# Latent attention's query projection without duplicated rotary columns, in a two-layer transformer trunk on one Trainium2 core

## The chip, the core and the metric

The kernel runs on one core of a Trainium2 chip. The core's engines run instruction streams of their own: PE (TensorE) multiplies matrices and transposes, DVE (VectorE), ACT (ScalarE) and POOL (GpSimd) work on tiles element by element, SP (SyncE) issues the DMAs. They wait for one another by semaphores. The metric is the device time of one execution in microseconds (us).

## The reference

Two layers over 256 tokens of 1024 numbers, all in fp32. Each layer mixes tokens in two groups of eight heads (latent attention and a sparse attention), then does a cross attention and a gated feed-forward. What matters here is the latent attention:

```python
q = (rms_norm(cq, cq_g) @ w_uq).reshape(B, S, 8, 64 + 32)
q_nope = q[..., :64]
q_rope = apply_rope(q[..., 64:], cos, sin)
s = (einsum('bqhd,bkhd->bhqk', q_nope, k_nope)
     + einsum('bqhd,bkd->bhqk', q_rope, k_rope)) * 96 ** -0.5

def apply_rope(x, cos, sin):
    x1, x2 = split(x, 2, axis=-1)          # 16 and 16
    return concatenate([x1 * c - x2 * s, x1 * s + x2 * c], axis=-1)
```

The query projection `w_uq` has 384 rows and 8 x 96 columns; the rotated part of the key is one for all heads.

## The kernel before

Every fp32 product is made of three matmuls: each operand is split into a high part (`hi`, by ACT, L130) and the rest (`lo`, by DVE, L131, which reads the raw tile and the high part), and hi x hi, lo x hi and hi x lo are added in PSUM (L177 to L179 where the weights stand still and the tokens move, L169 to L171 the other way). Weights come in by DMA, a piece at a time, into four raw buffers; the split pieces turn in six `hi` and six `lo` buffers.

A layer's attention is a list of named steps, written out by hand for each layer; the instructions of each step go to the engines in the order in which a list scheduler puts them, fixed before the run. In the two layers the end of the list reads

```
layer 0: ch qk3 kr mq2 mq0 fill mkv par2 mq1 mq3 av3 mqk2 mqk3 mqk0 mqk1 mav0 mav1 fill mav3 mav2
layer 1: ch av2 qk3 kr mq0 mkv mq3 mq1 av3 mqk0 mq2 mqk1 mqk3 mav0 mav3 mqk2 mav1 mav2
```

`mq0` to `mq3` (`mla_q`) project the queries of two heads each into `qT[g]`, where g is the group of four heads: pairs 0 and 1 make group 0, pairs 2 and 3 group 1. `mkv` makes keys (`kT`) and values, `kr` the rotary part of the keys. `mqk0` to `mqk3` (`mla_qk`, L721 and L722) are the scores and softmax of two heads each, `mav` their product with the values. `av3` is the last step of the sparse attention: transpositions of its probabilities (`pt`, L561), copies of them to SBUF (tag `pT`, four buffers, L564 on ACT and L566 on DVE), and products with the values (`pv`, L570 and L571, with `vsl` and then `vwn`). `fill` is work of the cross attention (keys and values of the memory), placed among the rest.

In `mla_q` a head takes 128 columns: 64 without rotation, the 32 rotary ones, and the two rotary halves of 16 once more, swapped. Each pair of heads has one raw piece of 3 x 192 columns, three splits on ACT and three on DVE into 3 x 256 columns, two chains of nine matmuls of 128x256, and one multiplication on DVE (L713) by the table `c_cs`, which holds ones, cosines and sines. The scores then contract over all 128 rows: the keys carry their rotated 32 rows twice (L404), so the product adds the two halves of the rotation.

## Time and profile before

| what | value |
|---|---|
| time of three runs, median (lowest to highest) | 888.48 us (885.98 to 889.66) |
| profiled execution, span | 887.0 us |
| mean granted clock of PE | 0.995 |
| matmuls of a query projection (L177 to L179, tile `mla`) | 18 per pair of heads, 72 per layer |
| multiplications by `c_cs` (L713) | 8 |
| POOL's instructions | 60 |

The profiled execution is one run of its own; the profile gives its span from the first to the last instruction and no other time for it. Busy times in a profile are sums over instructions, and matmuls overlap in the records, so that what a matmul takes in a sequence is read from the chain or from the starts. An engine's row in a window says how much of that stretch it worked.

### The profile page before, as it was taken

The page shows a single profiled execution, that of the slowest core. Times are in us where ns is not written, and L with a number is a line of the kernel's source. Part 1 is how long each engine was busy: PE and PEld are TensorE (multiplying, and loading weights), DVE is VectorE, ACT ScalarE, POOL GpSimd, SP SyncE. Part 2 cuts the span into 40 slices and gives each one's busy share as a digit, 9 for nine tenths or more (in the row PEclk, how much of TensorE's full clock was granted, in tenths as well). Part 3 has the DMA queues.
Part 4 walks back from the last instruction along what each step waited for, and adds up shares of the span by engine and source line. Part 5 has one row for each costly group of instructions (what it writes and reads, how often), then busy time and mean ns, then how long its engine had stood idle before and what let it go on. Part 6 is the DMA issues. An engine that isn't in the chain of part 4 may idle for free.

```text
span 887.0 us, 15857 instructions
## 1 busy us (share of the span) xinstructions
PE 857.6 (97%) x6088; PEld 794.2 (90%) x6088; DVE 659.9 (74%) x1293; ACT 511.7 (58%) x938; POOL 44.8 (5%) x60
## 2 busy tenths in 40 slices
PE   3999999999999999999999999999999999999996
PEld 3989798899989999999989998879998899999995
DVE  6788887766587777677687788868566877767767
ACT  4669764545545565465555678636573476555551
POOL 1053100000000000000000020000000000000000
PEclk9999999999999999999999999999999999999998
DMA  8954463485247656556537734546633746656631
GB/s 243 301 154 122 130 188 99 144 260 166 95 143 238 190 178 208 184 167 206 176 119 199 216 90 109 143 131 212 192 116 110 236 149 205 200 161 188 214 122 48
DMA packets 128523, 149.76 MB, mean 169 GB/s; under 512 B 6289, under 2 KB 111039, under 8 KB 128447
## 3 DMA queue, kind: packets, MB, share of 16 engines
q1 hardware_dynamic: 128447, 148.75, 54.6%
q8 instruction: 48, 0.79, 0.4%
q14 instruction: 28, 0.23, 0.1%
HBM read 147.68 MB, written 1.05 MB: 168 GB/s over the span
## 4 chain that ended last, share of the span: by engine, by line
PE 88%; DVE 5%; DMA 3%; ACT 2%; issue 1%; SPq 0%; POOL 0%; DVEq 0%; ACTq 0%; POOLq 0%
PE up L179 9%; PE up L178 9%; PE up L177 9%; PE acc L947 4%; PE acc L948 4%; PE acc L949 4%; PE acc L170 3%; PE acc L169 3%; PE acc L171 3%; PE fill L171 2%; PE xq L179 2%; PE xq L178 2%; PE xq L177 2%; PE fill L169 2%; PE fill L170 2%; PE pt L561 2%
## 5 line engine op out<-in xcount | busy, mean ns | idle before, releaser
L131 DVE TENSOR_TENSOR lo<-raw,hi 128x1024 fp32r<-128x1024 f32 (+5 forms) x296 | 320.6, 1096 | 82.9 <-ACT hi L130 78.3
L130 ACT ACTIVATE hi<-raw 128x1024 fp32r<-128x1024 f32 (+5 forms) x296 | 279.7, 957 | 152.7 <-PE acc L171 34.6
L179 PE MATMUL up<-xTh,lo 128*128 128x256 f32 x672 | 190.2, 283 | 0.0
L178 PE MATMUL up<-xTl,hi 128*128 128x256 f32 x672 | 190.2, 283 | 0.0
L177 PE MATMUL up<-xTh,hi 128*128 128x256 f32 x672 | 190.2, 283 | 0.0
L178 PEld LDWEIGHTS up<-xTl,hi 128*128 128x128 f32 x672 | 128.9, 192 | 0.7
L177 PEld LDWEIGHTS up<-xTh,hi 128*128 128x128 f32 x672 | 128.9, 192 | 0.7
L179 PEld LDWEIGHTS up<-xTh,lo 128*128 128x128 f32 x672 | 128.9, 192 | 0.0
L931 DVE SCALAR_TENSOR_TENSOR cv<-up,par,cv 128x255 f32<-128x255 f32 x88 | 42.1, 479 | 51.6 <-ACT cv L930 51.5
L930 ACT ACTIVATE cv<-up,par 128x256 f32<-128x256 f32 x88 | 49.0, 559 | 52.6 <-PE up L179 48.0
L948 PE MATMUL acc<-lo,frh 128*128 128x512 f32 x176 | 68.8, 391 | 0.0
L947 PE MATMUL acc<-hi,frh 128*128 128x512 f32 x176 | 68.7, 392 | 0.0
L949 PE MATMUL acc<-hi,frl 128*128 128x512 f32 x176 | 68.2, 389 | 0.0
L548 ACT ACTIVATE p<-p,nm 128x128 f32<-128x128 f32 (+1 forms) x96 | 42.8, 450 | 9.5 <-DVE nm L545 9.3
L199 POOL TENSOR_TENSOR mv<-mv,mhalf 128x1 f32<-128x1 f32 x16 | 14.7, 920 | 650.5 <-DVE mv L223 497.6
L932 DVE SCALAR_TENSOR_TENSOR cv<-up,par,cv 128x254 f32<-128x254 f32 x88 | 42.0, 479 | 1.4
L937 ACT ACTIVATE frh<-cv 128x256 fp32r<-128x256 f32 x44 | 18.3, 419 | 37.8 <-DVE cv L935 37.6
L949 PEld LDWEIGHTS acc<-hi,frl 128*128 128x128 f32 x176 | 33.0, 188 | 7.5 <-DVE frl L938 0.6
L947 PEld LDWEIGHTS acc<-hi,frh 128*128 128x128 f32 x176 | 33.1, 188 | 6.9 <-ACT frh L937 0.8
L177 PE MATMUL projt<-xTh,hi 128*128 128x256 f32 x128 | 37.2, 292 | 1.9 <-DVE c2l L462 1.6
L948 PEld LDWEIGHTS acc<-lo,frh 128*128 128x128 f32 x176 | 33.1, 188 | 6.0
L178 PE MATMUL projt<-xTl,hi 128*128 128x256 f32 x128 | 37.0, 289 | 0.5 <-DVE xTl L240 0.5
(257 smaller groups left out, 2027.6 us busy)
## 6 DMA issues: line engine op xcount, KB each, us to landing
raw<-in_ffn_w_up SPq DMA_DIRECT2D x88, 512.0 KB, 4.9
raw<-in_ffn_w_down SPq DMA_DIRECT2D x44, 512.0 KB, 4.3
raw<-in_xa_wkv SPq DMA_DIRECT2D x32, 512.0 KB, 4.3
raw<-in_xa_wq SPq DMA_DIRECT2D x16, 512.0 KB, 4.6
raw<-in_xa_wo SPq DMA_DIRECT2D x16, 512.0 KB, 4.1
raw<-in_w_in SPq DMA_DIRECT2D x24, 256.0 KB, 4.8
raw<-in_w_out SPq DMA_DIRECT2D x16, 256.0 KB, 5.4
raw<-in_w_out SPq DMA_DIRECT2D x8, 512.0 KB, 5.1
```

Source lines behind the costliest of these rows:

```text
L130: A.activation(h_, x_, AF.Copy)
L131: V.tensor_tensor(l_, x_, h_.bitcast(F32), op=ALU.subtract)
L169: T.matmul(o, xh_[:, t, k], h, start=k == 0, stop=False)
L170: T.matmul(o, xh_[:, t, k], lo, start=False, stop=False)
L171: T.matmul(o, xl_[:, t, k], h, start=False, stop=k == len(ws) - 1)
L177: T.matmul(o, h[:, ms], xh_[:, :, k], start=k == 0, stop=False)
L178: T.matmul(o, h[:, ms], xl_[:, :, k], start=False, stop=False)
L179: T.matmul(o, lo[:, ms], xh_[:, :, k], start=False, stop=k == len(ws) - 1)
L930: A.activation(c, u, AF.Identity, bias=pcol("cb", l, ft), scale=w_[2])
L947: T.matmul(o, fh[:, ts_], h[:, cs_], start=f == 0, stop=False)
L948: T.matmul(o, fh[:, ts_], lo[:, cs_], start=False, stop=False)
L949: T.matmul(o, fl[:, ts_], h[:, cs_], start=False, stop=f == NF - 1)
```

## The change

The duplicated columns go. A pair of heads projects its 2 x 64 columns without rotation in nine matmuls, and the 4 x 32 rotary columns of a group of four heads form one tile of 128 columns of their own, projected in nine matmuls by the second pair of the group. Their split weights (`rhi`, `rlo`) are filled in two halves, one by each pair, and hold a `hi` and a `lo` buffer from the first pair to the second. The 64 rows of each head go from PSUM to `qT` by a copy (ACT for one head of the pair; for the other DVE in a group's first pair and ACT in its second). The rotary tile is rotated by a shuffle of the partitions by 16 within each block of 32 (DVE), a multiplication by the cosines (`rc`, DVE), one of the shuffled tile by the signed sines (`rs`, POOL), and four additions of 32x256, in turn on POOL and DVE. `rc` and `rs` are buffers of the tag `pT`. The scores contract over 96 rows, the keys carry the rotated rows once, and `c_cs` has two tables of 256 columns.

```diff
-    cs = np.ones((P, S), f)
-    cs[64:80], cs[80:96] = cos.T, cos.T
-    cs[96:112], cs[112:128] = -sin.T, sin.T
+    cs = np.stack([np.tile(np.concatenate([cos.T, cos.T]), (4, 1)), np.tile(np.concatenate([-sin.T, sin.T]), (4, 1))], 1)
...
-                G.tensor_copy(kr[:, t, 96:128], kr[:, t, 64:96])
...
-                    V.tensor_copy(kT[g][64:128], pb[64:128, None, 0:S].to_broadcast([64, 4, S]))
+                    V.tensor_copy(kT[g][64:96], pb[64:96, None, 0:S].to_broadcast([32, 4, S]))
...
         def mla_q(ch, hp):
-            r2 = lambda v: v.rearrange("p k (h c) -> p (k h) c", h=2)
-            cols = [(lambda v: r2(v), lambda v: r2(v)[:, :, 0:96]),
-                    (lambda v: r2(v)[:, :, 80:96], lambda v: r2(v)[:, :, 96:112]),
-                    (lambda v: r2(v)[:, :, 64:80], lambda v: r2(v)[:, :, 112:128])]
-            ws = wmat(a["mla_w_uq"][l], [(hp * 192, (hp + 1) * 192)], ks=3, cols=cols, wn=256)
+            g, i = divmod(hp, 2)
+            last = g in rw
+            if not last:
+                rw[g] = [wp.tile([P, 3, P], F32R, name="r" + s, tag=s, bufs=HL) for s in ("hi", "lo")]
+            rh, rl = rw[g]
+            r = wp.tile([P, 1024], F32, name="raw", tag="raw", bufs=RAW)
+            rv = r[:, :576].rearrange("p (k n) -> p k n", k=3)
+            nc.sync.dma_start(rv, a["mla_w_uq"][l][:, hp * 192:(hp + 1) * 192].rearrange("(k p) n -> p k n", p=P))
+            h, lo = [wp.tile([P, 3, P], F32R, name=s, tag=s, bufs=HL) for s in ("hi", "lo")]
+            heads = lambda v: v.rearrange("p k (h c) -> p k h c", h=2)
+            ms = slice(64 * i, 64 * i + 64)
+            for cut, dh, dl in ((slice(0, 64), h, lo), (slice(64, 96), rh[:, :, ms], rl[:, :, ms])):
+                src, dh, dl = heads(rv)[:, :, :, cut], heads(dh), heads(dl)
+                A.activation(dh, src, AF.Copy)
+                V.tensor_tensor(dl, src, dh.bitcast(F32), op=ALU.subtract)
             pb = bank("mla")
-            for i in range(2):
-                mm_tr(pb[:, i * S:(i + 1) * S], ch[0], ch[1], ws, i * P)
-            j = 2 * (hp % 2)
-            V.tensor_tensor(qT[hp // 2][:, j:j + 2, :], pb.rearrange("p (i n) -> p i n", i=2),
-                            cs[:, None, :].to_broadcast([P, 2, S]), op=ALU.mult)
+            mm_tr(pb[:, 0:S], ch[0], ch[1], [(h[:, k], lo[:, k]) for k in range(3)], 0)
+            if last:
+                mm_tr(pb[:, S:2 * S], ch[0], ch[1], [(rh[:, k], rl[:, k]) for k in range(3)], 0)
+            A.activation(qT[g][0:64, 2 * i, :], pb[0:64, 0:S], AF.Copy)
+            copy_(qT[g][0:64, 2 * i + 1, :], pb[64:128, 0:S], i)
+            if last:
+                del rw[g]
+                rc, rs = [tmp.tile([P, S], F32, name=n, tag="pT", bufs=4) for n in ("rc", "rs")]
+                V.stream_shuffle(rs, pb[:, S:2 * S], [(c + 16) % 32 for c in range(32)])
+                V.tensor_tensor(rc, pb[:, S:2 * S], cs[:, 0], op=ALU.mult)
+                G.tensor_tensor(rs, rs, cs[:, 1], op=ALU.mult)
+                for j in range(4):
+                    js = slice(32 * j, 32 * j + 32)
+                    (G, V)[j % 2].tensor_tensor(qT[g][64:96, j, :], rc[js], rs[js], op=ALU.add)
...
-                T.matmul(b0[:, 0:P], qT[g][:, j, 0:P], kT[g][:, j, 0:P], start=True, stop=True)
-                T.matmul(b0[:, P:P + S], qT[g][:, j, P:S], kT[g][:, j, :], start=True, stop=True)
+                T.matmul(b0[:, 0:P], qT[g][0:96, j, 0:P], kT[g][0:96, j, 0:P], start=True, stop=True)
+                T.matmul(b0[:, P:P + S], qT[g][0:96, j, P:S], kT[g][0:96, j, :], start=True, stop=True)
```

The order moves with it at three places. First DVE in layer 0, between the projections `mq1` and `mq3` and the first softmax step (L545, in the changed kernel L542). Before; the splits `lo` of 128x1024 belong to the output weights:

```order
L131 TENSOR_TENSOR lo<-raw,hi 128x1024
L713 TENSOR_TENSOR qT_1340<-mla,c_cs 128x512
L131 TENSOR_TENSOR lo<-raw,hi 128x1024
L713 TENSOR_TENSOR qT_1341<-mla,c_cs 128x512
L131 TENSOR_TENSOR lo<-raw,hi 128x1024
L566 COPY pT<-pt 128x384
L131 TENSOR_TENSOR lo<-raw,hi 128x1024
```

After:

```order
L129 TENSOR_TENSOR lo<-raw,hi 128x1024 x2
L728 STREAM_SHUFFLE rs<-mla 128x256
L729 TENSOR_TENSOR rc<-mla,c_cs 128x256
L733 TENSOR_TENSOR qT_1338<-rc,rs 32x256 x2
L129 TENSOR_TENSOR lo<-raw,hi 128x1024
L728 STREAM_SHUFFLE rs<-mla 128x256
L729 TENSOR_TENSOR rc<-mla,c_cs 128x256
L733 TENSOR_TENSOR qT_1339<-rc,rs 32x256 x2
L563 COPY pT<-pt 128x384
L129 TENSOR_TENSOR lo<-raw,hi 128x1024
```

Two splits now stand together ahead of the rotation of group 0, a third between the two rotations, and one behind the copy `pT`; each rotation ends in two additions that read what POOL has multiplied.

Second POOL in layer 0, from the key's rotary part to the statistics of the next layer norm (L199, after L197). Before:

```order
L631 MEMSET pc 128x512
L402 MEMSET kr 128x64 x2
L199 ISA
L199 TENSOR_TENSOR mv<-mv,mhalf 128x1 x2
L447 MEMSET kk_160 64x512
```

After:

```order
L400 MEMSET kr 128x64 x2
L730 TENSOR_TENSOR rs<-rs,c_cs 128x256
L733 TENSOR_TENSOR qT_1338<-rc,rs 32x256 x2
L730 TENSOR_TENSOR rs<-rs,c_cs 128x256
L733 TENSOR_TENSOR qT_1339<-rc,rs 32x256 x2
L197 TENSOR_TENSOR mv<-mv,mhalf 128x1 x2
```

POOL had nothing to do between the two; now a multiplication and two additions for each group of heads stand there.

Third PE in layer 1, from the last projection `mq2` to the scores of heads 6 and 7 (`mqk3`). Before, `qT_6439` and `qT_6440` being the two groups' queries:

```order
L178 MATMUL mla<-xTl,hi 128x256
L179 MATMUL mla<-xTh,lo 128x256
L721 MATMUL mqk<-kT_6441,qT_6439 128x128
L722 MATMUL mqk<-kT_6441,qT_6439 128x256
L721 MATMUL mqk<-kT_6441,qT_6439 128x128
L722 MATMUL mqk<-kT_6441,qT_6439 128x256
L721 MATMUL mqk<-kT_6442,qT_6440 128x128
L722 MATMUL mqk<-kT_6442,qT_6440 128x256
L721 MATMUL mqk<-kT_6442,qT_6440 128x128
L722 MATMUL mqk<-kT_6442,qT_6440 128x256
```

After, where the groups are `qT_6435` and `qT_6436`:

```order
L175 MATMUL mla<-xTh,rhi 128x256
L176 MATMUL mla<-xTl,rhi 128x256
L177 MATMUL mla<-xTh,rlo 128x256
L740 MATMUL mqk<-kT_6437,qT_6435 128x128
L741 MATMUL mqk<-kT_6437,qT_6435 128x256
L740 MATMUL mqk<-kT_6437,qT_6435 128x128
L741 MATMUL mqk<-kT_6437,qT_6435 128x256
L558 MATMUL pt<-c_ident,p 128x128 x6
L740 MATMUL mqk<-kT_6438,qT_6436 128x128
L741 MATMUL mqk<-kT_6438,qT_6436 128x256
L740 MATMUL mqk<-kT_6438,qT_6436 128x128
```

The scores of group 1 came after two heads of group 0; now six transpositions stand there too, and these scores read the rotation of the tile that the nine `rhi` and `rlo` matmuls ahead have made.

## Rows read from the trace of the kernel before

**Rows 1.** Page, part 1: busy us of each engine, its share, instructions.

```profile
PE 857.6 (97%) x6088; PEld 794.2 (90%) x6088; DVE 659.9 (74%) x1293; ACT 511.7 (58%) x938; POOL 44.8 (5%) x60
```

**Rows 2.** Waits of PE, whole program: total us, times, longest.

```profile
PE pt L561 <- ACT pT L564: 1.7, 3, 0.8
```

**Rows 3.** Windows, layer 0: start:end us, busy by engine, granted clock, DMA share, GB/s.

```profile
110.00:117.00 7.00, 7.00 (x61) 7.00 (x60) 6.94 (x20) 3.71 (x9) 0.00 (x0) 1.00 0.08 11
117.00:128.00 11.00, 11.00 (x84) 10.23 (x84) 8.50 (x13) 7.27 (x11) 0.00 (x0) 1.00 0.89 241
128.00:136.00 8.00, 8.00 (x57) 6.45 (x54) 7.15 (x36) 6.11 (x22) 0.00 (x0) 1.00 0.65 189
```

**Rows 4.** Chain that ended last, layer 0: start us, us, what.

```profile
107.79 0.12 PE mla L178
...
121.89 0.14 PE mla L177
...
126.11 0.12 PE mla L179
...
126.23 1.31 PE pt L561 x12
...
127.54 0.63 PE pv L570 x4
```

**Rows 5.** DVE's groups by form: busy us, mean ns, idle before.

```profile
L131 DVE TENSOR_TENSOR lo<-raw,hi 128x1024 fp32r<-128x1024 f32 x228 | 277.8, 1222 | 79.7 <-ACT hi L130 75.4
...
L131 DVE TENSOR_TENSOR lo<-raw,hi 128x512 fp32r<-128x512 f32 x24 | 15.5, 686 | 0.3 <-ACT hi L130 0.3
...
L131 DVE TENSOR_TENSOR lo<-raw,hi 128x576 fp32r<-128x576 f32 x10 | 7.6, 762 | 0.0
...
L713 DVE TENSOR_TENSOR qT<-mla,c_cs 128x512 f32<-128x512 f32 x8 | 5.5, 690 | 1.1 <-PE mla L179 0.9
...
L131 DVE TENSOR_TENSOR lo<-raw,hi 128x96 fp32r<-128x96 f32 x16 | 3.4, 259 | 0.0
...
L533 DVE TENSOR_TENSOR oTl<-pv,oTh 128x256 fp32r<-128x256 f32 x8 | 3.4, 422 | 3.1 <-ACT oTh L532 3.0
```

**Rows 6.** ACT's groups by form, same columns.

```profile
L564 ACT ACTIVATE pT<-pt 128x384 f32<-128x384 f32 x28 | 12.2, 493 | 3.8 <-PE pt L561 3.5
...
L532 ACT ACTIVATE oTh<-pv 128x256 fp32r<-128x256 f32 x8 | 3.1, 386 | 5.5 <-PE pv L654 5.4
```

**Rows 7.** POOL's groups by form, same columns.

```profile
L623 POOL TENSOR_TENSOR sc<-sc,c_cok 128x256 f32<-128x256 f32 x2 | 1.7, 827 | 0.0
L621 POOL TENSOR_TENSOR sc<-sc,cmx 128x256 f32<-128x256 f32 x2 | 1.2, 623 | 52.2 <-DVE sm L552 49.2 <-DVE cmx L619 2.9
```

**Rows 8.** Timeline of POOL around 88 us: start us, us, instruction, idle before.

```profile
88.40 3.64 POOL L403 TENSOR_TENSOR kr<-m 128x32 f32<-128x32 f32 x1 [2.39 <-DVE m L401]
92.11 0.21 POOL L404 COPY kr<-kr 128x32 f32<-128x32 f32 x1
```

**Rows 9.** Timeline of DVE in the same stretch.

```profile
88.22 3.71 DVE L131 TENSOR_TENSOR lo<-raw,hi 128x96 fp32r<-128x96 f32 x7
```

**Rows 10.** Timeline of DVE ahead of layer 0's key/value matmuls.

```profile
113.79 3.23 DVE L131 TENSOR_TENSOR lo<-raw,hi 128x576 fp32r<-128x576 f32 x7
```

**Rows 11.** Chain that ended last, layer 1, same columns as rows 4.

```profile
561.83 1.31 PE pt L561 x12
...
569.26 0.43 PE mqk L722 x2
...
569.91 0.43 PE mqk L722 x2
...
571.66 0.66 PE pt L561 x6
```

**Rows 12.** Windows, layer 1, same columns as rows 3.

```profile
554.00:564.00 10.00, 10.00 (x78) 9.31 (x78) 9.67 (x18) 6.72 (x11) 0.00 (x0) 1.00 0.36 78
```

**Rows 13.** Instructions of the tile c_cs: ns min/median/max, first and last start us.

```profile
L293 SPq DMA_DIRECT2D c_cs<-in_c_cs x1: 445/445/445, 41.6 to 41.6; - x1
```

15 lines of the change are left out of this document (8 added, 7 removed).

## The prediction

> **What bounds the kernel now.** I read the busy line of the page first: TensorE (PE) is busy in 857.6 of 887.0 us, VectorE (DVE) in 659.9, ScalarE (ACT) in 511.7, GpSimd (POOL) in 44.8 [rows 1]. The reader should see an engine with 29.4 us of idle time in all. Then the waits of PE: the view has ten rows, nearly all at the layer norms and projections; the one below is the only one of a line that the latent-attention stretch uses too (a transposition of probabilities), 1.7 us in three places of the whole program, and no row waits at the scores' lines L721 or L722 [rows 2]. So where the query projection stands, nothing holds PE up: a matmul less is time less, and any new wait is time more. The windows of layer 0 say how near the next engine is: from 110 to 117 us PE is busy 7.00 and DVE 6.94 of 7, from 117 to 128 DVE 8.50 of 11, from 128 to 136 DVE 7.15 of 8; the granted clock is 1.00 throughout, the upper of its two levels [rows 3]. DVE keeps pace with PE there only just.
>
> **What is removed.** In the chain that ended last, a projection matmul of 128x256 gives 0.12 us [rows 4]. The change takes 18 of them away in each layer: a pair of heads had 18, it now has 9, and every second pair has 9 more for the rotary tile of its group of four heads. That is 18 x 0.12 = 2.16 us per layer, 4.3 us in all: the ceiling of the gain, 0.49% of 888.5 us.
>
> On DVE a pair loses a split of 0.76 us (128x576), two of 0.26 (128x96) and a multiplication of 0.69 [rows 5]: 1.97 x 4 = 7.9 us per layer. It gains splits of 128x384 and 128x192, by interpolation between those two rows 0.56 and 0.36 us: 3.7 us per layer. It gains per layer two copies 64x256, two shuffles 128x256, two multiplications 128x256 and four additions 32x256. None of these is in the trace; the nearest is the 128x256 operation on a PSUM bank at 0.42 us [rows 5], which I take for each (10 x 0.42 = 4.2 us). Bounds: 0.26 (128x96) and 0.69 (512 columns). DVE thus comes out even (7.9 for 7.9), and ACT has room, 7.27 of 11 us in the busiest of those windows [rows 3]; its six new copies cost about 0.39 each, as the 128x256 one does [rows 6]. So the engines' totals settle nothing; the order does.
>
> The shuffle alone has a price on a page. The Trainium skill, "VectorE: DVE Perf Modes", section "The perf-mode tier table (the rule you actually need)", gives some 2400 ns for 2048 columns at any permutation; pro rata, an estimate from that page, 256 columns are 0.30 us, and the sum below would be 0.5 us lower by it (four shuffles). No run here shows one yet.
>
> **What is added on the path.** The rotary half of the queries now goes through a chain: last rope matmul, shuffle (DVE), multiplication by the sines (POOL), two additions one after the other (POOL; two more on DVE). POOL at 128x256 needs 0.62 us (L621) to 0.83 (L623) [rows 7]; I take 0.62 for the multiplication and for an addition too, since it has as many columns (lower bound 0.21, the small copy in [rows 8]). With 0.1 us for each of four hand-overs, the chain is 0.42 + 3 x 0.62 + 0.4 = 2.7 us, the first addition 2.0. Before, one multiplication of 0.69 stood there. The cover it had is the same as it has now: what PE does between the last projection and the first score.
>
> A second thing rides on it. The shuffled and the multiplied tile take two of the four "pT" buffers, which hold the transposed probabilities. The dependencies of the new program make the ACT copy of the first transposed tile wait for the second POOL addition of the first group, and the fourth one for that of the second group. PE's value products are queued behind.
>
> And a third: the rope splits hold two of six split buffers from the first pair of a group to the second, so the four 128x512 splits of the key/value weights move from before the scalings of the probabilities to behind them.
>
> **Layer 0, place by place.** *(a)* PE comes to the key/value matmuls 2.16 us earlier, at about 113.6 us, and DVE has 2.7 us of splits (4 x 0.69, [rows 5]) to do after the scalings, which ended at 113.8 [rows 10] and now end perhaps 0.5 earlier. The order of PE puts the terms with the high parts first. Wait 0 to 1.2, I take 0.4. *(b)* The 36 matmuls of the last two pairs ran from 121.9 to 126.2 [rows 4]; now as many, 1.8 earlier: 120.1 to 124.5, the first rope tile ready at 122.3. Plus 2.7 for the chain and 0.6 for a split of 1.22 us [rows 5] in front of the shuffle (half of one, on average) and another 0.6 that a split costs POOL (below), plus 0.49 for the ACT copy [rows 6]: 126.7. PE, through with its twelve transpositions, is there at 125.8. Wait 0 to 2.5, I take 1.2. *(c)* The second shuffle is queued on DVE behind a multiplication, two additions that wait for POOL, and a split. The first scores read head 4, POOL's first addition, and the window's value products the last pT copy: 0 to 2.0, I take 1.0. *(d)* Two splits of the output weights (2.4 us) that stood ahead of the scores now stand among the softmax steps, in a stretch in which DVE had 0.85 of 8 us free [rows 3]: 0 to 1.6, I take 0.8. Layer 0: -2.16 + 0.4 + 1.2 + 1.0 + 0.8 = +1.2 us.
>
> **Layer 1.** All 18 matmuls go ahead of the first scores. *(e)* The first rope tile is ready at 561.83 - 2.16 + 0.66 (six transpositions moved ahead of it) = 560.3 [rows 11]; head 0 needs POOL's first addition, 560.3 + 2.0 + 0.6 = 562.9, and PE, which had finished its transpositions at 563.14 and has 0.85 us of value products next, is there at about 562.2 with the ACT copy they wait for. Wait 0 to 1.5, 0.8. *(f)* Before, the scores behind the last projection read queries that were made earlier; now one rotary tile of the last group serves heads 4 to 7. Between it and the scores of head 6 PE has two heads (0.65 us each, by the starts of their matmuls) and six transpositions (0.66) [rows 11], 1.96 us; head 6 needs a copy of the nope part on DVE (0.42), the chain (2.7), and half a split (0.6): 3.7. Wait 0.6 to 2.7, I take 2.0 for what DVE, 9.67 of 10 us busy just before [rows 12], may be late. Layer 1: -2.16 + 0.8 + 2.0 = +0.6 us.
>
> The rest costs nothing: the larger table of cosines is fetched at 41.6 us [rows 13], some 80 us before its first use, the shorter contraction of the scores (96 rows, not 128) leaves their columns alone, and the key's copies keep their 1024 columns.
>
> **Sum:** -4.3 + 6.2 = +1.9 us. The profiled execution spans 887.0 us, 0.17% under the median of 888.48, inside the runs' spread of 885.98 to 889.66; so 888.9 in its terms, and **890.4 us** as a median. All waits at their lower bounds: -3.7; at the upper ones: 1.2 + 2.5 + 2.0 + 1.6 + 1.5 + 2.7 - 4.3 = +7.2. A change under 0.5% (4.4 us) can hardly be told from none here.
>
> **The port, and where the traces bear on it.** A POOL addition of 128x32 took 3.64 us where it met DVE at seven splits in a row, 3.71 us long, each with two SBUF inputs [rows 8, 9]; the copy after it took 0.21. POOL came free when the run of splits ended. The new chain puts six POOL operations per group of heads beside such splits. The Trainium skill, "SBUF — State Buffer", section "SBUF: two separate sides", has the two engines share a port pair as an exclusive lock, held for one instruction by whichever started first, against DVE operations with two SBUF inputs. By that rule POOL could lose one split of 1.2 us at most each time; the row shows the loss of a whole run, and here the measurement decides.
>
> **The rivals.** *Hidden* (0.18): shuffle and additions come at their lower bounds (0.26 and 0.21; chain 1.5 us), everything is ready when PE arrives, and the 4.3 us stay: 884.2. For it: POOL is idle in these stretches, PE never waited there before. Against: (f) has 1.96 us of cover only, and a DVE copy ahead of the chain. *Port* (0.22), the other side: in each of the four chains POOL loses one split more than the half that I count, 4 x 1.22 = 4.9: 895.3. It decides from about 4 us between a shuffle and the second POOL addition. For it: the 3.64 us; splits stand directly behind the additions in the order. Against: between shuffle and split stand the PSUM multiplication and two additions that wait for POOL, which may let it through. *Softmax on DVE* (0.10): the splits of (d) delay all softmax steps of layer 0, 2.4 instead of 0.8, and PE's transpositions with them: 892.0. My forecast has 0.50, its own range 887 to 893.5.
>
> **From the cases to the numbers.** Half of "hidden" lies beyond 0.5%: faster 0.09. "Port" and the tail of "softmax" and of the forecast: slower 0.25. The rest, 0.66, is within 0.5%. The range, 884.0 to 896.0, runs from all waits hidden to the port's price with the upper bounds.
>
> **What would show it.** PE 4.3 us less busy and 6052 matmul rows instead of 6088; new rows among PE's waits at the score line, from POOL, and at the value products, from ACT's pT copies, one to two us each; in layer 1 a gap ahead of the last pair's scores of about 2 us; a shuffle near 0.42 us, POOL's operations near 0.62 where they meet no split. I am wrong if PE shows no such gap (then the time is 884), or if the POOL rows average over 1 us (then it is 893 or more), or if the clock falls below 1.00 in a gap and the matmuls behind it slow down.

## The result, and the profile after

The changed kernel takes 900.22 us (four runs, 897.52 to 902.94) where the kernel before takes 887.98 us beside it (885.98 to 889.66): 1.0133 [1.0111, 1.0156], 12.2 us slower. Its profiled execution spans 895.7 us and is the fastest of the four, 897.52 us. The forecast was 890.4 us with a range to 896.0, so that the change is slower than forecast by 9.8 us and lies outside the range.

Part 1 of the page of the changed kernel answers to [rows 1]:

```profile
span 895.7 us, 15831 instructions
...
PE 860.9 (96%) x6052; PEld 792.7 (89%) x6052; DVE 662.5 (74%) x1301; ACT 512.4 (57%) x942; POOL 50.0 (6%) x68
```

There are 36 matmuls less, as forecast, and yet PE is busy 3.3 us more. Matmuls fewer in number and longer in sum: that is the first sign. The waits of PE in the changed kernel (us in total, times, longest), for [rows 2]:

```profile
PE pv L567 <- ACT pT L561: 4.5, 3, 2.9
PE mqk L740 <- POOL qT L733: 4.1, 3, 2.1
PE pt L558 <- ACT pT L561: 1.9, 3, 0.8
```

Two rows are new, the two that the forecast named: value products behind ACT's copy of the probabilities, scores behind POOL's addition. The windows of layer 0, columns and first three stretches as in [rows 3], and the two stretches behind them:

```profile
110.00:117.00 7.00, 7.00 (x52) 6.56 (x51) 6.50 (x16) 3.44 (x8) 0.00 (x0) 1.00 0.37 114
117.00:128.00 11.00, 8.11 (x62) 7.04 (x60) 8.05 (x15) 7.43 (x13) 2.86 (x4) 0.98 0.82 216
128.00:136.00 8.00, 6.62 (x25) 4.45 (x25) 6.08 (x16) 3.84 (x9) 2.09 (x3) 0.50 0.61 159
136.00:141.00 5.00, 5.00 (x20) 4.46 (x19) 3.84 (x23) 3.87 (x16) 0.00 (x0) 0.50 0.17 64
141.00:150.00 9.00, 9.00 (x65) 8.04 (x64) 5.99 (x26) 4.36 (x14) 0.00 (x0) 0.99 0.41 117
```

The second column is PE. It loses 2.89 us before 128 and 1.38 behind it. Then the column that was 1.00 in [rows 3] falls to 0.50, the lower of the two clock levels, and stays there to about 141 us, although PE is busy throughout from 136 on: 20 matmuls in 5 us. The chain that ended last, layer 0 of the changed kernel, says what came late (start us, us, what):

```profile
114.96 5.58 DMA raw<-in_xa_wkv
120.64 1.07 ACT hi L128
...
122.89 0.46 DVE rs L728 x2
123.41 0.73 POOL rs L730
...
125.23 0.82 POOL qT L733
...
127.62 0.73 POOL rs L730
128.43 0.96 POOL qT L733
129.43 0.80 PE mqk L740 x2
```

Read from the top: a weight of the cross attention lands at 120.5 us, ACT and DVE split it, and only then can DVE take up the shuffle behind that split in its queue. PE had started the last matmul of group 0's rotary tile at 119.96 (its record ends at 120.25). In the order before, the splits in this place were those of the output weights; the cross attention's weights had been issued at 96.63 and 102.85, now at 113.00 (the stretch of the account below starts at 102.8 us before and at 100.9 now). DVE's timeline shows the queue:

```profile
121.73 1.23 DVE L129 TENSOR_TENSOR lo<-raw,hi 128x1024 fp32r<-128x1024 f32 x1 [1.40 <-ACT hi L128]
...
122.89 0.45 DVE L728 STREAM_SHUFFLE rs<-mla 128x256 f32<-128x256 f32 x1
...
124.17 1.28 DVE L733 TENSOR_TENSOR qT<-rc,rs 32x256 f32<-32x256 f32 x2 [0.53 <-POOL rs L730]
125.48 1.63 DVE L129 TENSOR_TENSOR lo<-raw,hi 128x1024 fp32r<-128x1024 f32 x1
127.05 0.01 DVE L728 LOAD_MASK_SELECT rs<-mla  x1
```

In layer 1 the chain of the changed kernel passes through the rotation of group 1 in the same way, and the window behind it has the lower clock for a while:

```profile
576.58 0.46 DVE rs L728
577.11 0.74 POOL rs L730
...
578.93 0.82 POOL qT L733
579.79 0.49 PE mqk L740 x2
```

```profile
580.00:585.00 5.00, 5.00 (x20) 4.24 (x20) 4.42 (x25) 3.18 (x14) 0.00 (x0) 0.66 0.36 120
```

What the new operations cost, from DVE's and POOL's groups by form in the changed kernel (columns as in [rows 5]):

```profile
L733 DVE TENSOR_TENSOR qT<-rc,rs 32x256 f32<-32x256 f32 x8 | 5.0, 630 | 2.1 <-POOL rs L730 2.0
...
L728 DVE STREAM_SHUFFLE rs<-mla 128x256 f32<-128x256 f32 x4 | 1.8, 446 | 0.1
...
L733 POOL TENSOR_TENSOR qT<-rc,rs 32x256 f32<-32x256 f32 x8 | 7.0, 876 | 0.6
L730 POOL TENSOR_TENSOR rs<-rs,c_cs 128x256 f32<-128x256 f32 x4 | 2.9, 726 | 48.7 <-DVE rs L728 47.1 <-issue 1.6
```

**The account.** I cut each layer from the first transposition of the latent (tile `cht`) to the first query matmul of the cross attention (tile `xq`). In windows of half a us through that stretch, idle is the length less PE's busy time, and the clock loss is the busy time times one minus the granted clock. Before, the stretches take 87.1 and 75.5 us, with 0.0 and 0.1 of idle and no clock loss. After, they take 96.3 (+9.2) and 78.7 (+3.2): idle 4.3 and 3.5, clock loss 6.1 and 1.7. So 12.4 us more = 7.7 of waits + 7.8 of clock - 3.1 for the rest. In the rest stand the matmuls that are gone: by their starts, the projection's matmuls take 2.19 us less in layer 0 and 2.15 in layer 1.

The 12.4 us are more than the two profiled executions differ by, 8.7 us (895.7 against 887.0). The one of before was slower elsewhere: it reached its first stretch at 102.8 us where the change was there at 100.9 (its clock was at 0.50 from 52.7 to 56.1 us, behind a wait of 1.7 us at a transposition of the tile `cmp`; in the profile of the change it wasn't), and it took 1.9 us more between the stretches. So that the 12.4 come so near the 12.2 us of the medians is partly luck.

The clock's part has a second witness: the changed kernel's four executions have a mean clock of 0.987 to 0.988; those of before, in the same sets and in later ones, 0.994 to 0.999. The middle of both ranges is 0.9 points apart, and 0.009 x 897 is 8 us.

### The profile page after: what moved, and what is told of

It reads as the page before. It is cut to its first block, busy times and chain, and to the rows that moved or that the text cites. A ratio compares the mean times of both kernels' runs of the same rounds, so it can differ in the third digit from the quotient of the medians.

```text
span 895.7 us, 15831 instructions
## 1 busy us (share of the span) xinstructions
PE 860.9 (96%) x6052; PEld 792.7 (89%) x6052; DVE 662.5 (74%) x1301; ACT 512.4 (57%) x942; POOL 50.0 (6%) x68
## 3 DMA queue, kind: packets, MB, share of 16 engines
q1 hardware_dynamic: 128447, 148.88, 53.5%
## 4 chain that ended last, share of the span: by engine, by line
PE 85%; DVE 6%; DMA 3%; ACT 2%; issue 2%; POOL 1%; SPq 0%; DVEq 0%; ACTq 0%; POOLq 0%
PE up L177 9%; PE up L176 9%; PE up L175 9%; PE acc L966 4%; PE acc L967 4%; PE acc L968 4%; PE acc L169 3%; PE acc L168 3%; PE acc L167 3%; DVE lo L129 2%; PE fill L169 2%; PE fill L167 2%; PE xq L177 2%; PE xq L176 2%; PE xq L175 2%; PE fill L168 2%
## 5 line engine op out<-in xcount | busy, mean ns | idle before, releaser
L129 DVE TENSOR_TENSOR lo<-raw,hi 128x1024 fp32r<-128x1024 f32 (+4 forms) x272 | 312.5, 1156 | 86.2 <-ACT hi L128 81.9
L128 ACT ACTIVATE hi<-raw 128x1024 fp32r<-128x1024 f32 (+4 forms) x272 | 270.8, 1003 | 153.9 <-PE acc L169 31.9
L197 POOL TENSOR_TENSOR mv<-mv,mhalf 128x1 f32<-128x1 f32 x16 | 15.4, 961 | 602.3 <-DVE mv L221 497.6
L545 ACT ACTIVATE p<-p,nm 128x128 f32<-128x128 f32 (+1 forms) x96 | 42.6, 446 | 8.8 <-DVE nm L542 8.5
L175 PE MATMUL fill<-mTh,hi 128*128 128x256 f32 x128 | 37.5, 293 | 0.0
```

Of the source, the lines that this page charges most:

```text
L128: A.activation(h_, x_, AF.Copy)
L129: V.tensor_tensor(l_, x_, h_.bitcast(F32), op=ALU.subtract)
L175: T.matmul(o, h[:, ms], xh_[:, :, k], start=k == 0, stop=False)
```

## The experiments

Two theories stood against each other after the result: that the waits alone make the loss, through one resource (the `pT` buffers, the held split buffers, POOL, or the order of the steps), and that a large part is the clock that falls behind them. Each expectation names its own. All edits below are to the changed kernel unless the text says "before"; "L0" and "L1" are the two stretches of the account, as differences to before in the profiled execution, with idle and clock loss in brackets.

| kernel | us | ratio to before | L0 (idle, clock) | L1 (idle, clock) |
|---|---|---|---|---|
| the change | 900.22 | 1.0133 [1.0111, 1.0156] | +9.2 (4.3, 6.1) | +3.2 (3.5, 1.7) |
| own_pt | 900.24 | 1.0119 [1.0104, 1.0134] | +1.5 (3.0, 0) | +8.7 (3.7, 3.1) |
| keep_busy | 899.99 | 1.0110 [1.0093, 1.0127] | +8.6 (3.7, 4.3) | +3.2 (3.5, 1.7) |
| no_rot | 894.53 | 1.0060 [1.0044, 1.0077] | +5.0 (4.5, 1.6) | +2.2 (1.6, 0) |
| reorder | 891.54 | 1.0033 [1.0018, 1.0047] | +2.6 (2.3, 0) | +1.2 (3.0, 0) |
| ro_split | 896.53 | 1.0084 [1.0060, 1.0108] | +2.9 (2.5, 0) | +6.3 (2.6, 5.1) |
| ro_split_pt | 891.99 | 1.0038 [1.0023, 1.0053] | +1.9 (1.6, 0) | +2.7 (1.2, 0) |
| dve_only | 898.95 | 1.0125 [1.0103, 1.0146] | +4.3 (3.5, 1.7) | +6.9 (3.6, 1.7) |
| fewer_mm (before) | 881.25 | 0.9916 [0.9890, 0.9941] | -2.2 (0.4, 0) | -3.0 (0, 0) |
| hold2_before (before) | 892.73 | 1.0044 [1.0026, 1.0063] | +1.0 (0, 0) | +2.6 (1.9, 0) |
| chain_before (before) | 891.64 | 1.0028 [1.0011, 1.0045] | +2.9 (2.0, 1.7) | +0.1 (0.7, 0) |
| reorder_own | 891.16 | 1.0031 [1.0016, 1.0045] | +1.1 (1.5, 0) | +2.3 (1.7, 0) |
| reorder_b | 895.65 | 1.0100 [1.0080, 1.0120] | +2.9 (3.4, 0) | +6.3 (2.9, 0) |
| no_wait | 903.67 | 1.0158 [1.0115, 1.0202] | +14.8 (3.8, 11.8) | +1.9 (0.8, 0) |
| no_wait_own | 899.83 | 1.0120 [1.0073, 1.0167] | +12.0 (2.6, 10.2) | +6.8 (1.8, 3.4) |
| busy_gaps | 899.99 | 1.0146 [1.0120, 1.0171] | +7.9 (3.8, 2.7) | +3.2 (3.5, 1.7) |
| busy_all | 899.26 | 1.0111 [1.0090, 1.0133] | +3.8 (0.2, 0) | +3.2 (2.0, 0) |

The ratios are to runs of the kernel before on the same chip in the same set (its medians were 886.92 to 889.60). Idle counts the time in which no matmul's record runs; a projection matmul's record lasts 0.28 us and the next starts after 0.12, so that a short wait shows less idle time than it costs.

### own_pt: the rotation's temporaries in a buffer of their own

```diff
-                rc, rs = [tmp.tile([P, S], F32, name=n, tag="pT", bufs=4) for n in ("rc", "rs")]
+                rcs = tmp.tile([P, 2, S], F32, name="rcs", tag="hs", bufs=1)
+                rc, rs = rcs[:, 0], rcs[:, 1]
```

> The two rotary temporaries get a buffer of their own, so no copy of transposed probabilities waits for them. Theory A (the pT buffers hold PE up): PE's 2.9 us wait at the value products of layer 0 goes, its clock stays up more often, 893 to 897 us. Theory B (the rotated queries themselves are late, since the shuffle is queued on VectorE behind splits and three GpSimd operations follow): PE only waits one step later, at the first scores, until the same GpSimd addition near 129.4 us; 899 to 901 us.

900.24 us: nothing won. The waits of PE in this kernel show why:

```profile
PE mqk L741 <- POOL qT L734: 5.3, 3, 2.8
...
PE pv L567 <- ACT pT L561: 1.9, 2, 1.0
```

The value products wait 2.6 us less, the scores 1.2 more. Layer 0 is now nearly as fast as before (+1.5), with 3.0 us idle and the clock at 1.00 all the way; in layer 1 the scores' wait is followed by the low clock:

```profile
575.00:580.00 5.00, 2.90 (x9) 2.55 (x10) 2.98 (x13) 3.68 (x13) 1.90 (x3) 0.64 0.50 158
580.00:585.00 5.00, 5.00 (x19) 3.86 (x18) 3.59 (x17) 1.20 (x6) 0.00 (x0) 0.68 0.00 0
```

A wait for a late tile isn't removed by freeing one of its consumers; the next one in PE's queue takes it over.

### keep_busy: 27 matmuls whose result is overwritten, in layer 0 ahead of the transpositions

```diff
+            if last and l == 0 and hp == 3:
+                for n in range(3):
+                    mm_tr(bank("mla")[:, 0:S], ch[0], ch[1], [(rh[:, k], rl[:, k]) for k in range(3)], 0)
```

> 27 more matmuls of 128x256 (3.2 us) in layer 0, whose result nobody reads, stand where PE had its 2.9 us gap ahead of the value products. Theory C (most of the loss is the lower clock after the gap, 0.50 for some 13 us): the granted clock from 128 to 141 us is 1.00 or nearly so, and the kernel is 3 to 6 us faster than the changed one, 894 to 897 us, though PE does more. If the waits alone were the loss: 900 to 903 us, since the extra work fills a gap and shortens nothing.

899.99 us, a miss. The first gap was filled (value products wait 0.2 there), but the two places behind it opened instead, 1.6 us at the scores and 1.9 at the next value product, and the clock fell behind those:

```profile
128.00:136.00 8.00, 4.32 (x32) 3.28 (x32) 7.32 (x11) 4.36 (x7) 3.99 (x5) 0.86 0.44 128
136.00:141.00 5.00, 5.00 (x21) 3.35 (x18) 3.21 (x10) 1.57 (x6) 0.00 (x0) 0.50 0.94 270
```

### no_rot: four copies in place of the rotation

```diff
-                rc, rs = [tmp.tile([P, S], F32, name=n, tag="pT", bufs=4) for n in ("rc", "rs")]
-                V.stream_shuffle(rs, pb[:, S:2 * S], [(c + 16) % 32 for c in range(32)])
-                V.tensor_tensor(rc, pb[:, S:2 * S], cs[:, 0], op=ALU.mult)
-                G.tensor_tensor(rs, rs, cs[:, 1], op=ALU.mult)
...
-                    (G, V)[j % 2].tensor_tensor(qT[g][64:96, j, :], rc[js], rs[js], op=ALU.add)
+                    A.activation(qT[g][64:96, j, :], pb[js, S:2 * S], AF.Copy)
```

> The rotation of the queries is left out: four copies on ScalarE take the rotary columns from PSUM to the queries as they are; projection, splits and buffers are those of the changed kernel. Theory B (shuffle, GpSimd and additions are late): nearly all the loss goes, 883 to 886 us, the 4.3 us of matmuls show as gain. Rival D (the split buffers that the rotary weights hold, and the later weight transfers, cost by themselves): 888 to 894 us, with waits of PE left in the projection stretch.

894.53 us, better than the change but still slower than before, and no clean test: in layer 0 the value products wait 4.5 us, for ACT copies that stand behind the new ACT copies and behind splits of the late weights. The rotation is then not the only thing late; the weights are too.

### reorder: both projections of a group next to one another

The two pairs of a group follow one another in both layers (lists cut to the steps that move):

```diff
-layer 0: mq2 mq0 fill mkv par2 mq1 mq3 av3
+layer 0: mq2 mq3 fill mkv par2 mq0 mq1 av3
-layer 1: mq0 mkv mq3 mq1 av3 mqk0 mq2 mqk1 mqk3
+layer 1: mq0 mq1 mkv mq3 mq2 av3 mqk0 mqk1 mqk3
```

> The two pairs of a group of heads are projected one after the other (layer 0: pairs 2, 3 before the filling work, 0, 1 behind; layer 1: 0, 1, then keys and values, 3, 2), so one group is rotated long before its scores and only one group's rotary weights are held at a time. Theory B: the waits at the scores shrink to those of one group, under 2 us in layer 0, the clock stays near 1.00, 886 to 892 us. Theory A: the wait for the pT buffers stays 2 to 3 us in layer 0 and the clock falls again, 896 to 900 us.

891.54 us: nearly nine of the twelve us come back. The buffers are held for a shorter time, one group is rotated long before it is needed, waits shrink (the longest, at a value product, is 1.5 us), and the clock is 1.00 in both stretches.

### ro_split, ro_split_pt and reorder_own: the same order with buffers freed

The first adds buffers of their own for the split rotary weights, the second for the temporaries as well, the third for the temporaries alone (its edit to `rc` and `rs` is that of own_pt):

```diff
-                rw[g] = [wp.tile([P, 3, P], F32R, name="r" + s, tag=s, bufs=HL) for s in ("hi", "lo")]
+                rw[g] = [pl.tile([P, 3, P], F32R, name="r" + s, tag=tg, bufs=1) for s, pl, tg in (("hi", tmp, "hs"), ("lo", st, "pc"))]
...
-                rc, rs = [tmp.tile([P, S], F32, name=n, tag="pT", bufs=4) for n in ("rc", "rs")]
+                rc, rs = [st.tile([P, S], F32, name=n, tag=tg, bufs=1) for n, tg in (("rc", "sc"), ("rs", "gev"))]
```

> The reordered kernel, and the rotary weights' splits in two buffers of their own (1.5 KB each, tags that are idle in this stage), so that all six hi and lo buffers turn as before. Theory D: a further 2 to 4 us under reorder's 891.5, so 886 to 889.5 us, with the in_xa_wkv transfers out before 105 us. Theory B: as reorder, 890 to 892.5 us.

> As ro_split, and the two rotary temporaries in buffers of their own too. Theory A (the pT buffers still cost, now that the rest is in time; reorder waits 3.7 us at value products): 1 to 3 us under ro_split, 884 to 887 us, the ceiling of the matmul saving being 883.7. If the pT buffers cost nothing then: within 0.8 us of ro_split.

> The reordered kernel with the rotary temporaries in a buffer of their own; the rotary splits stay among the six. Of reorder's waits, 3.7 us stand at value products that wait for pT copies; if the temporaries cause them (theory A): 887 to 889.5 us, even with the kernel before or a little under. If ScalarE and VectorE are simply late there (rival E): 890.5 to 892 us, as reorder.

896.53, 891.99 and 891.16 us; the first two are above what was expected, the third is what its rival foresaw. In ro_split the cross attention's weights went out at 92.07 us, early as expected, and nothing was won by it. With one buffer set for both groups ro_split loses five us against reorder, all of it in layer 1, where a wait of 2.6 us is followed by a clock of 0.53 from 570 to 580 us. The last is the best version of the change that I found, with the waits in both stretches at 3.2 us together and the clock whole, as its windows show against those above:

```profile
117.00:128.00 11.00, 9.57 (x67) 8.26 (x66) 9.24 (x18) 5.93 (x12) 0.09 (x1) 1.00 0.77 193
128.00:136.00 8.00, 8.00 (x57) 6.56 (x53) 7.75 (x35) 6.65 (x21) 2.39 (x3) 1.00 0.75 196
```

It is still 0.3% slower than before, [0.16, 0.45], and waits don't explain that: the saved matmuls and 3.2 us of idle time would leave a gain of 1.1 us, where its stretches are 3.4 us longer. Part of it is the order of the value products of `mav` (tile `mpv`). Before, most pairs of heads have theirs side by side in PE's order, the matmuls of the two heads mostly start 0.013 to 0.014 us apart, and four run in the time of two; here most heads come one after the other (PE's timeline, first line and second: before, third: reorder_own):

```profile
578.02 0.66 PE L570 MATMUL mpv<-pT,vmla 128*64 128x256 f32 x4
...
580.33 0.65 PE L570 MATMUL mpv<-pT,vmla 128*64 128x256 f32 x2
...
575.34 0.65 PE L567 MATMUL mpv<-pT,vmla 128*64 128x256 f32 x2
```

Five of the eight pairs stand side by side before, six in the change, two in reorder_own, whose value products take 2.0 us more than before by their starts. No run tests this order by itself.

### reorder_b: all four projections together ahead of the keys

```diff
-layer 0: mq2 mq3 fill mkv par2 mq0 mq1 av3
+layer 0: mq2 mq3 mq0 mq1 fill mkv par2 av3
-layer 1: mq0 mq1 mkv mq3 mq2 av3
+layer 1: mq0 mq1 mq3 mq2 mkv av3
```

> All four projections of a layer stand together ahead of the filling work and the keys and values, and the temporaries have a buffer of their own, so both rotations have 5 us or more of cover in layer 0. Theory B: no wait for the rotation, clock 1.00; 885 to 889 us. Rival E (ScalarE and VectorE, which must now split all query weights early, set the pace): 890 to 894 us with waits ahead of the projections or the key matmuls.

895.65 us (the diff is against reorder_own). No rotation is late any more, but the splits of the other weights are: in layer 0 PE waits at six places, 0.2 to 0.9 us each, for splits and for copies of keys, values and probabilities. The clock is 1.00 throughout, so that waits lose time without it too: 6.3 us of idle time in the two stretches, which are 9.2 us longer. What else makes them longer isn't shown; the order of the value products is part of it, as in reorder_own.

### dve_only: the whole rotation on DVE

```diff
-                G.tensor_tensor(rs, rs, cs[:, 1], op=ALU.mult)
+                V.tensor_tensor(rs, rs, cs[:, 1], op=ALU.mult)
...
-                    (G, V)[j % 2].tensor_tensor(qT[g][64:96, j, :], rc[js], rs[js], op=ALU.add)
+                    V.tensor_tensor(qT[g][64:96, j, :], rc[js], rs[js], op=ALU.add)
```

> The changed kernel with the whole rotation on VectorE: GpSimd does nothing in it. Theory P (GpSimd's 0.73 and 0.9 us and its contention with VectorE's additions of 0.64 make the chain late): the chain from shuffle to last addition falls from about 3.3 to 2.2 us in all, twice per layer on the path: 894 to 897 us. Theory D or B by queueing (late splits ahead of the shuffle): 898 to 901 us.

898.95 us. The rotation itself gets a little shorter (2.8 us from shuffle to last addition in layer 0 where it was 3.2, the four additions taking 1.71 in sequence), but in layer 0 its shuffle starts at 125.85 us, behind a split that waits 2.32 us for ACT's high part. POOL's speed isn't what made the rotation late.

### fewer_mm, hold2_before and chain_before: one part of the change alone, in the kernel before

fewer_mm leaves out 16 projection matmuls per layer:

```diff
+        first = set()
...
-                mm_tr(pb[:, i * S:(i + 1) * S], ch[0], ch[1], ws, i * P)
+                if i and not hp // 2 in first:
+                    T.matmul(pb[:, S:2 * S], ws[0][0][:, P:2 * P], ch[0][:, :, 0], start=True, stop=True)
+                else:
+                    mm_tr(pb[:, i * S:(i + 1) * S], ch[0], ch[1], ws, i * P)
+            first.add(hp // 2)
```

> The kernel before with 16 of the 72 projection matmuls of a layer left out (the second head of each group's first pair gets one matmul instead of nine, so its queries are only approximate); no other instruction changes in kind. If PE bounds the stage, as the prediction's step said (a matmul less is time less): 32 x 0.12 = 3.8 us, 884.5 us. Rival E (VectorE, 6.94 of 7 us busy there, and ScalarE's transfers set the pace; the saving turns into new waits of PE): 887 to 888.5 us, with 2 to 4 us of new waits at pt, pv or mla.

881.25 us, a gain of 7.3 [5.2, 9.8] where the rows price 32 x 0.12 = 3.8 us. PE is busy 850.9 us on its page, and its one new wait is 0.3 us at a value product. That the projection is bound by PE holds, and so does the price. The busy time of the tile `mla` in the two stretches, before and in fewer_mm, is 3.84 us less for 32 matmuls, 0.12 each:

```profile
sum 162.55, PE 24.67; mean PE 12.34
...
sum 157.34, PE 20.83; mean PE 10.42
```

The gain beyond that is elsewhere. The stretches are 5.2 us shorter, 1.6 of it at the value products of `mav`, which stand side by side for more pairs of heads (see reorder_own); the rest of the 8.2 us between the two profiles lies outside the stretches, 1.8 of it ahead of the first.

hold2_before takes a `hi` and a `lo` buffer at a group's first pair and gives them back behind the second:

```diff
...
+            if not last:
+                rw[g] = [wp.tile([P, 1024], F32R, name="r" + s, tag=s, bufs=HL) for s in ("hi", "lo")]
+                V.memset(rw[g][0][0:1, 0:1].bitcast(F32), 0.0)
+                V.memset(rw[g][1][0:1, 0:1].bitcast(F32), 0.0)
...
+            if last:
+                for v in rw.pop(g):
+                    jk = st.tile([P, 1], F32, name="jkr", tag="ss")
+                    V.tensor_tensor(jk[0:1], v[0:1, 0:1].bitcast(F32), pb[0:1, 0:1], op=ALU.add)
```

> As hold_before, but the two held buffers are released only after the second pair's projection (the read that ends the hold now also reads the projection's result), as in the changed kernel; four tiny VectorE operations per layer are added. Theory D (the hold alone moves the key/value weights' splits behind the scalings and the in_xa_wkv transfers to 113 us): layer 0's stretch from the transpositions of the latent to the cross attention's queries, 87.1 us before, grows by 2 to 5 us. Theory B/A (late rotation and pT buffers): it stays within 0.7 us.

892.73 us. SP's timeline in this kernel shows the cross attention's weights issued late, 12.3 us behind the start of the stretch where it is 12.1 in the change:

```profile
116.15 1.60 SPq L122 DMA_DIRECT2D raw<-in_xa_wkv  x2
```

So the hold alone delays those weights; with nothing that needs the rotation behind them on DVE, it costs layer 0 only 1.0 us and no idle time, between what the two theories had (2 to 5 us, and within 0.7). Layer 1 is 2.6 us longer, with a wait of 0.6 us for one of the added operations themselves. (A first form of it, hold_before, gave the buffers back at 84.21 us already, before the hold mattered, and told nothing: 890.90 us, 1.0030 [1.0012, 1.0047], layer 0 unchanged. What was expected of that form:)

> The kernel before, in which each group of heads also holds one hi and one lo buffer from its first pair's projection to its second's, unused but for one element, as the changed kernel does for the rotary weights; nothing else is changed. Theory D (the held split buffers alone make the transfers of in_xa_wkv leave at 113 us instead of 97 to 103 and put late splits ahead of the rest): 891 to 895 us, that is 2 to 6 us slower than before, with splits of 128x1024 on ScalarE waiting for DMA near 118 us. Theory B (only the rotation is late): 888 to 889.5 us, as before.

chain_before runs the rotation's operations into a scratch tile that nobody reads, with the temporaries in `pT` buffers:

```diff
+        first = set()
...
+            if hp // 2 in first:
+                rc, rs = [tmp.tile([P, S], F32, name=n, tag="pT", bufs=4) for n in ("rc", "rs")]
+                o = st.tile([P, S], F32, name="scr", tag="sc", bufs=1)
+                V.stream_shuffle(rs, pb[:, S:2 * S], [(c + 16) % 32 for c in range(32)])
+                V.tensor_tensor(rc, pb[:, S:2 * S], cs, op=ALU.mult)
+                G.tensor_tensor(rs, rs, cs, op=ALU.mult)
+                for n in range(4):
+                    js = slice(32 * n, 32 * n + 32)
+                    (G, V)[n % 2].tensor_tensor(o[js], rc[js], rs[js], op=ALU.add)
+            first.add(hp // 2)
```

> The kernel before, which does the changed kernel's rotation as well, into a scratch tile that nobody reads: shuffle, multiplications and additions at the same places on VectorE and GpSimd, the temporaries in pT buffers; projection, splits and scores stay as before. Theory A (pT buffers held by the temporaries, and the time on VectorE): waits of PE at the value products of 2 to 4 us in layer 0, 891 to 896 us. If the loss needs the scores to wait for the rotation (theory B): 888.5 to 890 us.

891.64 us. With the weights on time (issued at 95.01 and 101.25 us) and no score that reads the rotation, the shared buffers make the value products wait all the same: ACT's copy waits for the last addition of the first rotation. The clock dips behind it (waits, then the window):

```profile
PE pv L570 <- ACT pT L564: 2.0, 1, 2.0
```

```profile
128.00:136.00 8.00, 8.00 (x43) 6.08 (x44) 7.30 (x23) 3.47 (x13) 3.56 (x3) 0.79 0.39 105
```

The three parts alone come to -0.84 + 0.44 + 0.28 = -0.12%; together they are +1.33%. (With 3.84 us for the matmuls, the price shown above, fewer_mm's part is -0.43% and the sum +0.29%; the copies of the 64 rows and the smaller splits stand in none of the three.) Most of the loss isn't in any of them but in how they meet: held buffers make weights late, late weights stand ahead of the shuffle, the shuffle's result is now what the scores and the `pT` buffers wait for.

### no_wait and no_wait_own: scores that don't read the rotation

```diff
-                T.matmul(b0[:, 0:P], qT[g][0:96, j, 0:P], kT[g][0:96, j, 0:P], start=True, stop=True)
-                T.matmul(b0[:, P:P + S], qT[g][0:96, j, P:S], kT[g][0:96, j, :], start=True, stop=True)
+                T.matmul(b0[:, 0:P], qT[g][0:64, j, 0:P], kT[g][0:64, j, 0:P], start=True, stop=True)
+                T.matmul(b0[:, P:P + S], qT[g][0:64, j, P:S], kT[g][0:64, j, :], start=True, stop=True)
```

The second has own_pt's edit too.

> The changed kernel, whose scores contract over the 64 rows without rotation only: the rotary part of the scores is left out, all of the rotation is still done and nobody waits for its result except through the pT buffers. If the waits of the scores for the rotated queries (4.1 us in the profile) and the clock behind them are what is lost: 890 to 894 us. If the pT buffers' wait in layer 0 (2.9 us) alone brings the clock down: 897 to 900 us.

> As no_wait, and the temporaries in a buffer of their own: nothing on PE waits for the rotation at all; projection, splits, held split buffers and all of the rotation's work stay. If the waits and their clock are the loss: 884 to 889 us, a gain of 4.3 us less what the held buffers and VectorE's queue cost. If the queues behind late weight transfers cost most: 892 us or more.

903.67 and 899.83 us: a wait less, and by the median not faster. no_wait has one wait left in layer 0, and its windows show the longest stretch of low clock of all:

```profile
PE pv L567 <- ACT pT L561: 5.5, 3, 3.8
```

```profile
128.00:136.00 8.00, 6.48 (x26) 4.16 (x26) 7.30 (x14) 3.75 (x7) 3.38 (x5) 0.58 0.35 117
136.00:141.00 5.00, 5.00 (x16) 3.78 (x14) 3.38 (x20) 4.27 (x15) 0.00 (x0) 0.50 0.73 209
141.00:150.00 9.00, 9.00 (x30) 6.82 (x30) 4.32 (x20) 2.52 (x10) 0.00 (x0) 0.50 0.13 30
```

Its four runs are the cleanest view of what the clock is worth, since the program is the same: 904.32, 904.59 and 903.01 us with a mean clock of 0.984, 0.984 and 0.987, and 894.67 us with 0.998. no_wait_own splits alike: 907.87 and 904.24 at 0.981 and 0.984, 895.41 and 895.14 at 0.997 and 0.995. Eight to thirteen us between executions of one program go with the clock; whether their waits were alike isn't known, since one of each four was profiled, with a low clock both times (904.32 and 907.87 us). The executions with the high clock, 894.67 to 895.41 us, are some five us faster than the change and still about eight slower than before (886.92 in their set).

In layer 0 of no_wait_own nothing on PE waits for the rotation, and yet the value products wait 2.5 us for ACT. Its timeline shows the late weights in a second queue, ahead of the copies of the probabilities:

```profile
125.04 1.06 ACT L128 ACTIVATE hi<-raw 128x1024 fp32r<-128x1024 f32 x1 [1.41 <-DMA raw<-in_xa_wkv]
...
127.48 1.06 ACT L128 ACTIVATE hi<-raw 128x1024 fp32r<-128x1024 f32 x1 [0.72 <-DMA raw<-in_w_out]
...
129.36 1.26 ACT L561 ACTIVATE pT<-pt 128x384 f32<-128x384 f32 x3
```

Between these stand the four new copies to `qT`, 0.36 to 0.38 us each. So by this timeline the late weights and the new copies delay PE in this order without the rotation, too.

### busy_gaps and busy_all: the gaps filled

Matmuls whose result is overwritten, in front of the waits: 24 and 12 in layer 0 for busy_gaps; for busy_all 24, 16 and 12 in layer 0 and 18 in layer 1.

```diff
+        def busy(o, n):
+            for k in range(n):
+                T.matmul(o[:, 0:S], mh[:, 0, k % 8], mh[:, :, k % 8], start=True, stop=True)
...
+            if l == 0 and j == 3:
+                busy(po, 24)
...
+                if l == 0 and j == 3 and br:
+                    busy(bank("fill"), 16)
...
+                if (l, hp) in ((0, 2), (1, 3)) and i == 0:
+                    busy(b0, 12 + 6 * l)
```

> The changed kernel with matmuls whose result is overwritten, placed in layer 0 where PE waits: 24 ahead of the value products (2.9 us), 12 ahead of the first scores (1.4 us). The waits are as long as before, but filled. Theory C (more than half of layer 0's loss is the clock): granted clock 1.00 from 128 to 141 us, layer 0's stretch falls from 96.3 to 90 to 92 us, the time to 893 to 896 us. If the clock falls all the same, or does not matter: 899 to 903 us.

> The changed kernel with matmuls that nobody reads in every long wait of PE: in layer 0 24 ahead of the value products, 16 between those with vsl and vwn, 12 ahead of the first scores; in layer 1 18 ahead of the scores of heads 6 and 7. That is 70 matmuls, 8.4 us of work more than the changed kernel. Theory C (the clock takes 7.8 us of the loss, as much as the waits): granted clock 1.00 in both stretches, 892 to 896 us, 4 to 8 us faster than the changed kernel though it does more. If the accounting is wrong and the waits alone are the loss: 900 to 904 us.

busy_gaps, 899.99 us, left the place between its two fillings open: a wait of 3.0 us at a value product behind DVE's `pT` copy, and a clock of 0.76 and 0.69 in the two windows from 128 to 141 us. busy_all has no idle time left there, and the clock stays up, as its windows show:

```profile
128.00:136.00 8.00, 7.87 (x66) 6.55 (x66) 6.72 (x10) 4.48 (x7) 2.91 (x4) 1.00 0.47 141
136.00:141.00 5.00, 5.00 (x34) 4.52 (x33) 4.98 (x27) 3.40 (x15) 0.00 (x0) 1.00 0.98 282
```

In layer 0 it makes 52 matmuls more, 6.2 us at 0.12, and the stretch is 5.5 us shorter than in the change (90.8 against 96.3): more work in less time. In layer 1 the 18 others bring nothing: the stretch is 78.7 us as in the change, with 2.0 of idle and no clock loss. The mean clock of its runs is 0.993 to 0.996. The whole program, 899.26 us where I expected 892 to 896, isn't faster beyond the noise: the intervals of its ratio and the change's overlap. In the two profiles (894.7 and 895.7 us) 4.4 of the 5.5 us are lost again outside the stretches. Layer 0's begins at 104.6 us instead of 100.9, ahead of every filling and with a clock of 0.50 from 53.5 to 56.9 us, and 0.7 us more pass between the stretches. So one profile shows what the low clock costs layer 0; the total times don't confirm it.

## Why the prediction was wrong

**The ceiling of the gain** (-4.3 us) held in mechanism and size: PE has 36 matmuls less, by their starts the projection takes 2.19 and 2.15 us less in the two layers (forecast 2.16 each), and the 32 that fewer_mm leaves out take 3.84 us.

**The waits** were right in place and about right in sum: 7.7 us where the forecast had 6.2. Place by place, forecast then measured: *(a)* key/value matmuls 0.4, 0; *(b)* value products of layer 0 1.2, 2.9; *(c)* scores of layer 0 1.0, 1.4; *(d)* softmax 0.8, no wait of its own; *(e)* first scores of layer 1 0.8, 1.3 (0.6 at the scores and 0.7 at the value products); *(f)* last pair 2.0, 2.1. The one that was clearly mis-sized is (b), and the step is "0.6 for a split of 1.22 us in front of the shuffle". It counted the split's length and not what the split waits for: from the start of the rotary tile's last matmul at 119.96 to the shuffle at 122.89 us pass 2.9 us, since the split waits for ACT, and ACT for weights that the held buffers have made late. The forecast saw that the hold moves splits, but followed the key/value weights only, not the cross attention's behind them.

**The step that failed** is the sum itself: -4.3 + 6.2 has no term for the clock. It was named, as a thing that would make the forecast wrong ("if the clock falls below 1.00 in a gap and the matmuls behind it slow down"), but got no price and no chance. It cost 7.8 us, as much as the waits: -4.3 + 7.7 + 7.8 = +11.2, against 12.4 in the stretches and 12.2 between the medians. Without it, at the same waits, the forecast's own terms give about 892.

**The rivals.** *Hidden* fell: nothing was ready in time, and the chain took 3.2 us (its own bounds give 0.26 + 3 x 0.21 + 0.4 = 1.3, not the 1.5 that it states). *Port* has the nearest time, 895.3, but not its mechanism: it was to decide from about 4 us between a shuffle and the second POOL addition, and by the chain that takes 3.2 in layer 0 (122.89 to 126.05) and 3.2 in layer 1 (576.58 to 579.75). POOL's addition does take 0.88 rather than 0.62 us, DVE's 0.63, and one split beside POOL's additions 1.63 instead of 1.22: they lose parts of one instruction to each other. The addition of [rows 8] takes 0.25 us in the change, but the 3.64 us did come again elsewhere: it takes 3.64 in fewer_mm and chain_before and 2.51 in both kernels with held buffers, beside such a run of splits. The Trainium skill, "SBUF — State Buffer", section "SBUF: two separate sides", has the two engines lock each other out for one instruction at a time; the rows of the rotation agree with it, and the row of before, a loss over seven splits, does not. dve_only, without POOL in the rotation, is no faster, so that the port isn't what made the loss. *Softmax on DVE* shows no row of its own.

**The shuffle** takes 0.446 us. I took 0.42 from the nearest row; the estimate from the Trainium skill, "VectorE: DVE Perf Modes", section "The perf-mode tier table (the rule you actually need)", was 0.30 pro rata. The row was nearer; on so short an operation the columns aren't the whole price, as the rows of before show for DVE's splits (0.26 us at 96 columns, 0.69 at 512).

**What stays open.** That idle time comes before the low clock is shown in each trace, and in layer 0 filling it keeps the clock up (busy_all). How much the clock loses isn't settled by how long PE waits in sum: 3.0 us idle in layer 0 of own_pt (two waits, 1.0 and 1.9) left it at 1.00, and 2.6 in that of no_wait_own (one wait of 2.5) brought 20.5 us at 0.50; two executions of one program differ by ten us. That the late weights make the rotation late is read from the chain, and hold2_before shows that the hold makes the weights late; the change in its own order with buffers of their own for `rhi` and `rlo` was not run. ro_split, which has them, has the other order, and wins nothing.

## What to carry to other kernels

Where one engine is busy 97% of the time, price a new wait twice: once as the wait, and once as what the matmuls behind it may cost at the lower clock, here as much again (7.7 and 7.8 us in the change; in reorder, with 5.3 us of idle time and no wait over 1.5, the clock stayed up). Before splitting one tile into parts that meet later, follow every tile that a held buffer delays to the in-order queue in which it will stand, and ask what is behind it: here DVE's queue, and ACT's as well. Then keep the parts close together and early in the order: that alone (reorder) won back nearly nine of the twelve us, where freeing single buffers moved the wait on.

## What the runs showed of the hardware that was not expected

After waits of 2.6 to 4.3 us in a stretch, PE's granted clock went to 0.50 and stayed there for 13.7 us in the change (fill matmuls start 0.21 us apart until about 141 us and 0.12 us apart from then on), and for 20.5 and 23.9 us in no_wait_own and no_wait, with PE busy without a gap through most of it. Busy again isn't at once fast again, and by its mean clock (0.984 and 0.998 in no_wait) the same program runs with or without it.

A POOL addition over only 32 partitions (32x256, 0.876 us) took longer than the multiplication over 128 (128x256, 0.726 us) in the same chain; the additions have a DVE addition beside them and the multiplication has not always, so that the runs don't tell how much of that is POOL's own.
